# Block products of a two-layer network on one Trainium2 core: part of VectorE's splits and residual adds handed to ScalarE and adding DMAs, two more block pairs, modulation kept off the last tiles

## The chip, the cores and the metric

The kernel runs on one core of one Trainium2 chip. Its engines are named as the profile names them: PE (TensorE; PEld are its weight loads), DVE (VectorE), ACT (ScalarE), POOL (GpSimd) and SP (SyncE, which here issues nearly all DMAs). The metric is the device time of one execution in microseconds (us), as a median over runs.

## The reference, cut to what matters

The network has two layers on 256 latent and 256 context tokens of width 1024. Each layer is a half-weighted gated feed-forward net (ffn), a mixer (a short convolution in layer 0, grouped-query attention in layer 1) and a second ffn. Every step normalises its input, scales and shifts it, and adds its output through a gate. Scale, shift and gate come from a modulation vector, one product per layer of the conditioning vector `c` with a 1024 x 9216 matrix.

```python
mod = (silu(c) @ mod_w[i] + mod_b[i]).reshape(3, 3, 1, 1024)     # shift, scale, gate of three steps
h   = rms(lat, norm_g) * (1 + mod_scale) + mod_shift
gte, up = split(h @ w13, 2)                                       # 1024 -> 2 x 2816
lat = lat + 0.5 * mod_gate * ((silu(gte) * up) @ w2)              # 2816 -> 1024
...                                                               # conv or attention, without the 0.5
```

The context tokens run through the same weights with their own modulation; in layer 1 only the latent tokens are needed after the attention.

## The kernel before, in words

The activations `x` stay in SBUF as 8 tiles of 128 rows (width) by 512 columns (tokens, latent then context). All products are done in a rounded f32 format: `split` (L107 to L109) makes a high part by an ACT copy and a low part by a DVE subtraction, and `mm3` (L128 to L133) multiplies high by high, high by low and low by high, three matmuls for each product.

An ffn with 512 tokens goes through its 22 hidden tiles in thirds of 8, 7 and 7. For each third come first the products with `w13` and the gate (`ffn`, L754), then `project` (L569), which multiplies by `w2` and adds the eight output tiles into `x` through `finish` (L547), two DVE operations for each tile (L553), one for each token stream. After the third third the tiles go on to `tail`, which squares them, sums the squares and prepares the next norm. Tiles 6 and 7 come last and by halves (`late`). There are three ffns with 512 tokens: (0,0), (0,1) and (1,0); the last, (1,1), has 256 tokens and another form.

A hidden tile of the first product is done in one of two ways. As it is: `w13_mm`, 48 matmuls of 512 columns. Or as a `Pair` (L675): seven block products instead of eight, made of sums of weight blocks and of activation blocks (A11, A12, S1 to S4, A22 against B or T1 to T4), 7 x 12 = 84 matmuls of 256 columns. A pair's weights are loaded by SP (two loads of 512 KB); `sums` (L696) forms S1 to S4 on DVE in place and splits all blocks. A22, the fourth product block, keeps its parts in `w4h` and `w4l` (two buffers each); they are used by `four`, a pair's last twelve matmuls, which run after the first products of the next pair. `AS_IS` (L25) says which tiles of the first third stay as they are; in ffn (0,0) tiles 3 to 7 do (tiles 0 to 2 are part of the written-out start), in the others none is named. At the end of a third the last pair's products `seven` and `four` are put between the first tiles of `project`.

The modulation vector is computed on DVE in 224 units (`mod_unit`, L162): an elementwise product with a running sum of a 128 x 1024 tile of the matrix (`junk`), fed by SP loads of `in_modT`, two loads of 512 KB for four units. `tick(n)` makes n units due; it is called behind each pair, as-is tile, output tile and in the attention stage. `mod_ready` runs all units that a vector still lacks. `gate_of` and `lazy_gate` fetch a whole gate at the first `finish` and multiply it by 0.5 for an ffn.

The start and the attention are written out by hand. Elsewhere a scheduler decides each engine's order, so the units of a `tick` needn't stand where it is called. Every engine's queue is run in order.

Of the kernel before, what the change touches and what calls it, by code (L numbers as in the profile page):

```python
# [9 lines left out]
F32 = mybir.dt.float32  # L10
# [11 lines left out]
NM = 22  # L22
THIRDS = (8, 7, 7)

AS_IS = {(0, 0): range(3, 8), (0, 1): (), (1, 0): ()}  # L25

EARLY = 4
HEADS = 8
# [19 lines left out]
def hybrid_kernel(ctx: ExitStack, tc: tile.TileContext, a: dict, out: bass.AP):  # L48
# [13 lines left out]
    def nm(s):  # L62
        uid[0] += 1
        return f"{s}{uid[0]}"
# [102 lines left out]
    def mod_unit(l, ch, pair, raw, j, v):  # L167

        mt = mod_tile(l, ch)
        kt = pair * 2 + j  # L170
        col = ch * KT + kt
        junk = mp.tile([P, D], BF16, name=nm("junk"), tag="junk", bufs=1)
        nc.vector.tensor_tensor_reduce(  # L173
            out=junk,
            in0=raw[j],
            in1=scbc[:, v, :],
            scale=1.0,
            scalar=modb[:, l, col : col + 1],
            op0=ALU.mult,
            op1=ALU.add,  # L180
            accum_out=mt[:, kt, v : v + 1],
        )
        done[l, ch] += 1

    def streams(l, ch):
        return 1 if l == 1 and ch >= 5 else 2
# [23 lines left out]
    def tick(n):  # L210

        owed[0] += n
        while (jobs or units) and owed[0] >= 1:
            owed[0] -= 1
            next_unit()

    def mod_ready(l, ch):
        while not ((l, ch) in done and done[l, ch] == 8 * streams(l, ch)):
            next_unit()
        return modv[l, ch]  # L220
# [10 lines left out]
        return t  # L231

    def gate_of(l, j):
        m = mod_ready(l, 3 * j + 2)
        if j == 1:
            return m
        t = const.tile([P, KT, 2], F32, name=f"G{l}{j}", tag=f"G{l}{j}")
        nv = 1 if (l, j) == (1, 2) else 2
        nc.vector.tensor_scalar(
            out=t[:, :, :nv], in0=m[:, :, :nv], scalar1=0.5, scalar2=None, op0=ALU.mult  # L240
        )
        return t


    accs = {}
# [299 lines left out]
        return tail  # L545

    def finish(m, ps, c0, c1, gate, tail, wide=False):  # L547
        g = gate()
        for s in range(2):
            for o in [s * S - c0] if not wide else range(0, T2 if s == 0 else 0, S):  # L550
                if not c0 <= s * S < c1:
                    continue
                nc.vector.scalar_tensor_tensor(  # L553
                    out=x[:, m, s * S : s * S + S],
                    in0=ps[:, o : o + S],
                    scalar=g[:, m, s : s + 1],
                    in1=x[:, m, s * S : s * S + S],
                    op0=ALU.mult,
                    op1=ALU.add,
                )  # L560
        if tail:
            tail(m, c0, c1)
# [6 lines left out]
    def project(ws, src, nk, gate, tail, tot, late, ev, between=()):  # L569

        def products(ps, w, ks, c0, c1, wide=True):
            ms = [src(k, c0, c1) for k in ks]
            if wide and len(ms[0]) == 3:
                return mm_wide(ps, [w(k) for k in ks], ms, ks[0] == 0, ks[-1] == nk - 1)
            for k, m in zip(ks, ms):  # L580
                mm3(ps[:, : c1 - c0], w(k), m[:2], k == 0, k == nk - 1)

        nf = 3 if between else 2
        ahead = {}

        def get(m):
            for i in range(m, min(m + 3, KT)):
                if i not in ahead:
                    ahead[i] = ws(i)
            return ahead[m]  # L590

        w2 = [get(m) for m in range(nf)]
        p2 = [psum("py") for _ in range(nf)]
        cut = nk - 2 if between else nk - 1
        for i in range(nf):
            products(p2[i], w2[i], range(cut), 0, tot)
            if i < len(between):
                between[i]()
        if between:
            for i in range(nf):  # L600
                products(p2[i], w2[i], (nk - 2,), 0, tot)
        for i in range(nf):
            products(p2[i], w2[i], (nk - 1,), 0, tot)
            finish(i, p2[i], 0, tot, gate, tail, len(src(0, 0, tot)) == 3)
            tick(ev)

        for m in range(nf, KT - late):
            if tail and tot == S and m == KT - 2:
                ready()
            w = get(m)  # L610
            ps = psum("py")
            wide = len(src(0, 0, tot)) == 3 and m < KT - 1
            products(ps, w, range(nk), 0, tot, wide)
            finish(m, ps, 0, tot, gate, tail, wide)
            tick(ev)
        if late:

            wl = [get(m) for m in (6, 7)]
            if tail:
                ready()  # L620
            for s in range(2):
# [53 lines left out]
    class Pair:  # L675
# [4 lines left out]


        def __init__(self, src, h):
            self.h, self.w = h, {}
            self.raw = [load_raw(src[:, c : c + 1024]) for c in (0, 1024)]
            ts = half()
            for i, key in enumerate(("A11", "A12")):
                self.w[key] = [t[:, i * T2 : i * T2 + T2] for t in ts]
                split(*self.w[key], self.raw[i][:, T2:])
# [7 lines left out]
        def sums(self, n):  # L696

            r1, r2 = self.raw
            s1, s2 = r1[:, :T2], r1[:, T2:]
            tt = nc.vector.tensor_tensor  # L700
            if n == 0:
                tt(out=s1, in0=s1, in1=r2[:, :T2], op=ALU.subtract)
                tt(out=s2, in0=s2, in1=s1, op=ALU.subtract)
                self.keep(("S1", "S2"), r1)
                return
            self.w["A22"] = [
                wp.tile([P, T2], F32R, name=nm(t), tag=t, bufs=2) for t in ("w4h", "w4l")
            ]
            split(*self.w["A22"], r2[:, :T2])
            v = lambda t: t.rearrange("p (a c) -> p a c", a=2)  # L710
            tt(  # L711
                out=v(r2), in0=v(r2), in1=s2.unsqueeze(1).to_broadcast([P, 2, T2]),
                op=ALU.subtract,
            )
            self.keep(("S3", "S4"), r2)
# [35 lines left out]
            nc.vector.tensor_tensor(out=self.gm, in0=self.sg, in1=self.u, op=ALU.mult)  # L751
            split(g[0], g[1], self.gm)

    def ffn(l, b, h, tot, gate, tail, gs=(), ev=1.5, z=None):  # L754
        gs = list(gs)
        i0 = 0
        for t, n in enumerate(THIRDS):
            between = ()
            if tot == T2:
# [22 lines left out]
                for i in range(len(gs), n):  # L782
                    if t == 0 and not heads and i in AS_IS[l, b]:
# [12 lines left out]
                        w13_mm(pp, w, h, range(4, KT), 0, T2)  # L796
                        gs.append(new_pair("g"))
                        w13_post(pp, gs[-1], 0, T2)
                        tick(4)
                        continue  # L800
                    if heads:
                        pr = heads.pop(0)
# [44 lines left out]
            def ws2(m):  # L847
# [10 lines left out]
                ws2,  # L858
                (lambda k, c0, c1: cur[k]) if tot == S
                else lambda k, c0, c1: (cur[k][0][:, c0:c1], cur[k][1][:, c0:c1]), n,  # L860
                gate, tail if end else None, tot, 2 if end and tot == T2 else 0, ev, between,
            )
            gs = []

    def lazy_gate(l, j):
        box = []

        def get():
            if not box:
                box.append(gate_of(l, j))  # L870
            return box[0]

        return get


    h = Plain()
# [170 lines left out]
    for i in range(3):  # L1047
        gs0.append(new_pair("g"))
        w13_post(pps[i], gs0[i], 0, T2)

    with tc.issue_after(rows["last"]):
        convk = cload("convk", [P, 3, KT])
        qg = cload("qg", [P, 1])
        kg = cload("kg", [P, 1])
        cosT = cload("cosT", [P, S])
        sinT = cload("sinT", [P, S])


    hn = Plain()
    ffn(0, 0, h, T2, lazy_gate(0, 0), tail_norm(0, 1, hn), gs0, 2)  # L1060
    h = hn

    zs = []
    for m in range(KT):
# [4 lines left out]
        for c0, c1 in ((0, S), (S, T2)) if m == 0 else ((0, T2),):  # L1069
# [11 lines left out]
        u = tp.tile([P, T2], F32, name=nm("u"), tag="gm", bufs=3)  # L1081
        nc.vector.tensor_tensor(out=u, in0=xv, in1=pc, op=ALU.mult)
        d = tp.tile([P, T2], F32, name=nm("d"), tag="gm", bufs=3)
        nc.vector.tensor_scalar(
            out=d, in0=u, scalar1=convk[:, 1, m : m + 1], scalar2=None, op0=ALU.mult
        )
# [11 lines left out]
        nc.vector.tensor_tensor(out=z, in0=d, in1=pb, op=ALU.mult)  # L1098
        zs.append(new_pair("z"))
        split(zs[m][0], zs[m][1], z)  # L1100
        tick(5)

    def by_pairs(key, box=None):
        box = box or {}
# [9 lines left out]
    hn = Blocks()  # L1114
    project(
        by_pairs("cw_out"), lambda k, c0, c1: (zs[k][0][:, c0:c1], zs[k][1][:, c0:c1]), KT,
        lazy_gate(0, 1), tail_norm(0, 2, hn), T2, 2, 1.5,
    )
    h = hn
    hn = Blocks()  # L1120
    ffn(0, 1, h, T2, lazy_gate(0, 2), tail_norm(1, 0, hn), (), 1.7)
    h = hn


    hn = Plain()
    ffn(1, 0, h, T2, lazy_gate(1, 0), tail_norm(1, 1, hn), (), 1.5)
    h = hn
    ap = ctx.enter_context(tc.tile_pool(name="ap", bufs=2))

# [210 lines left out]
    with tc.manual_schedule(engines={e.engine for e in (nc.tensor, nc.vector, nc.scalar, nc.gpsimd)}):  # L1340
# [29 lines left out]
    hn, hz = Beside(), Early()  # L1370
    roomy.append(True)
    project(
        by_pairs("wo", wos), lambda k, c0, c1: aos[k], KT, lazy_gate(1, 1), tail_early(1, 2, hn, hz), S, 0, 0,
    )
    ffn(
        1, 1, hn, S, lazy_gate(1, 2),
        lambda m, c0, c1: nc.sync.dma_start(out[m], x[:, m, :S]), z=hz,
    )

# [79 lines left out]
```

## Time and profile before

| | |
|---|---|
| median of three runs | 1569.89 us (1569.86, 1569.89, 1573.92) |
| the profiled execution | 1571.47 us, of which 1569.7 are the span |
| granted clock of PE, mean | 0.998 |
| PE busy | 1557.7 us, 99% of the span, 10210 matmuls |
| DVE busy | 1333.4 us, 85%, 2129 instructions |
| ACT busy | 733.8 us, 47%, 1213 instructions |
| POOL busy | 25.4 us, 2%, 20 instructions |
| DMA | 248.80 MB, mean 159 GB/s |

The busy share is an average over stages. Where an engine is not the last that the next step waits for, its idle or busy time says nothing of the end. In the rows of the profile, a line such as `L109 DVE TENSOR_TENSOR wl<-wr,wh 128x1024` is an operation of line 109 on DVE that writes `wl` from `wr` and `wh`. Behind it stand the count, the busy time in all, the mean in ns, and the idle time of the engine just before with what ended it. In a window row, each engine has its busy time and its count of instructions; PEclk is the granted clock of PE as a share of full speed.

### The profile page before, as it was taken

To read this page: it belongs to the slowest core of one execution; us is meant where nothing else is said; L and a number is where in the kernel's file an instruction comes from. 1 tells how busy PE (TensorE), PEld (TensorE's weight loads), DVE (VectorE), ACT (ScalarE), POOL (GpSimd) and SP (SyncE) were. 2 spreads that over 40 slices of the span, in tenths; PEclk is the share of its full clock that TensorE was granted. 3 is DMA by queue.
4 is the path that set the end of the run, shared out by engine and by line. 5 is a ranking of instruction groups with operands and counts; after the bars stand their busy time and mean duration, and the time that the engine had idled before them with its cause. 6 is when DMAs were issued, how large, how long until landed. Compare 5 with 4: busy or idle time off the path is not lost.

```text
span 1569.7 us, 25671 instructions
## 1 busy us (share of the span) xinstructions
PE 1557.7 (99%) x10210; PEld 1422.0 (91%) x10210; DVE 1333.4 (85%) x2129; ACT 733.8 (47%) x1213; POOL 25.4 (2%) x20
## 2 busy tenths in 40 slices
PE   9999999999999999999999999999999999999999
PEld 7888998999888899989899899999899889898888
DVE  5998789899997698978989989969978887887676
ACT  5622452545322365435345465435345445674553
POOL 0000000000000000000000000000000002300000
PEclk9999999999999999999999999999999999999999
DMA  9675246355565323542533614533733853366562
GB/s 373 224 237 180 89 132 187 107 173 159 194 209 166 114 75 108 177 146 87 189 126 117 196 41 135 187 108 118 239 112 114 265 154 106 123 207 221 171 199 75
DMA packets 72120, 248.80 MB, mean 159 GB/s; under 512 B 9024, under 2 KB 10816, under 8 KB 72000
## 3 DMA queue, kind: packets, MB, share of 16 engines
q1 hardware_dynamic: 69408, 245.40, 48.0%
q10 hardware_dynamic: 2592, 1.76, 0.4%
q8 instruction: 80, 1.31, 0.3%
q14 instruction: 40, 0.33, 0.1%
HBM read 244.77 MB, written 1.05 MB: 157 GB/s over the span
## 4 chain that ended last, share of the span: by engine, by line
PE 88%; DVE 6%; DMA 2%; ACT 2%; issue 1%; POOL 0%; POOLq 0%; SPq 0%; ACTq 0%; DVEq 0%
PE py L131 8%; PE py L132 8%; PE py L133 8%; PE p L131 6%; PE p L133 6%; PE p L132 6%; PE q L133 5%; PE q L131 4%; PE q L132 4%; PE py L139 2%; PE pu L139 2%; PE pg L139 2%; PE pg L132 1%; PE pg L133 1%; DMA wr<-in_w 1%; PE pu L132 1%
## 5 line engine op out<-in xcount | busy, mean ns | idle before, releaser
L108 ACT ACTIVATE wh<-wr 128x1024 fp32r<-128x1024 f32 (+2 forms) x442 | 393.7, 916 | 361.9 <-PE py L132 119.6
L109 DVE TENSOR_TENSOR wl<-wr,wh 128x1024 fp32r<-128x1024 f32 (+2 forms) x442 | 454.5, 1048 | 95.1 <-ACT wh L108 76.2
L173 DVE CUSTOM_DVE_ANT_0 junk<-wr,scbc,modb 128x1024 bf16<-128x1024 f32 x218 | 279.4, 1282 | 15.2 <-DMA wr<-in_modT 13.1
L131 PE MATMUL py<-gh,wh 128*128 128x512 f32 (+1 forms) x570 | 214.7, 377 | 0.0
L132 PE MATMUL py<-gl,wh 128*128 128x512 f32 (+1 forms) x570 | 214.0, 375 | 0.0
L133 PE MATMUL py<-gh,wl 128*128 128x512 f32 (+1 forms) x570 | 213.9, 375 | 0.0
L133 PEld LDWEIGHTS py<-gh,wl 128*128 128x128 f32 x570 | 108.3, 190 | 19.0
L131 PEld LDWEIGHTS py<-gh,wh 128*128 128x128 f32 x570 | 108.5, 190 | 18.4
L132 PEld LDWEIGHTS py<-gl,wh 128*128 128x128 f32 x570 | 108.5, 190 | 18.2
L131 PE MATMUL p<-th,wh 128*128 128x256 f32 x432 | 122.3, 283 | 0.0
L132 PE MATMUL p<-tl,wh 128*128 128x256 f32 x432 | 122.3, 283 | 0.0
L133 PE MATMUL p<-th,wl 128*128 128x256 f32 x432 | 122.2, 283 | 0.0
L553 DVE SCALAR_TENSOR_TENSOR x<-py,G,x 128x256 f32<-128x256 f32 x189 | 83.5, 479 | 36.3 <-PE py L133 25.1
L133 PE MATMUL q<-bh,wl 128*128 128x256 f32 x320 | 91.5, 286 | 0.1
L131 PE MATMUL q<-bh,wh 128*128 128x256 f32 x320 | 90.9, 284 | 0.4 <-ACT wh L108 0.4
L132 PE MATMUL q<-bl,wh 128*128 128x256 f32 x320 | 90.5, 283 | 0.0
L132 PEld LDWEIGHTS p<-tl,wh 128*128 128x128 f32 x432 | 82.8, 192 | 0.3
L131 PEld LDWEIGHTS p<-th,wh 128*128 128x128 f32 x432 | 82.8, 192 | 0.3
L133 PEld LDWEIGHTS p<-th,wl 128*128 128x128 f32 x432 | 82.8, 192 | 0.0
L108 ACT ACTIVATE w4h<-wr 128x512 fp32r<-128x512 f32 x54 | 33.8, 625 | 75.1 <-DMA wr<-in_w 56.9
L108 ACT ACTIVATE gh<-gm 128x512 fp32r<-128x512 f32 x66 | 41.6, 630 | 56.0 <-DVE gm L751 53.8
L711 DVE TENSOR_TENSOR wr<-wr,wr 128x1024 f32<-128x1024 f32 x54 | 66.0, 1222 | 0.7
(303 smaller groups left out, 3946.3 us busy)
## 6 DMA issues: line engine op xcount, KB each, us to landing
wr<-in_w SPq DMA_DIRECT2D x176, 512.0 KB, 4.5
wr<-in_modT SPq DMA_DIRECT2D x122, 512.0 KB, 4.5
wr<-in_w2b SPq DMA_DIRECT2D x64, 448.0 KB, 3.9
wr<-in_w2a SPq DMA_DIRECT2D x32, 512.0 KB, 4.7
pm<-in_mod SPq DMA_DIRECT2D x16, 512.0 KB, 10.2
wr<-in_cw_cx SPq DMA_DIRECT2D x16, 512.0 KB, 4.7
wr<-in_cw_b SPq DMA_DIRECT2D x8, 512.0 KB, 4.4
wr<-in_cw_out SPq DMA_DIRECT2D x8, 512.0 KB, 3.9
```

Source lines behind the costliest of these rows:

```text
L108: nc.scalar.activation(out=hi, in_=src, func=AF.Copy)
L109: return nc.vector.tensor_tensor(out=lo, in0=src, in1=hi.bitcast(F32), op=ALU.subtract)
L131: nc.tensor.matmul(ps, wh, mh, start=first, stop=False, **kw)
L132: nc.tensor.matmul(ps, wh, ml, start=False, stop=False, **kw)
L133: nc.tensor.matmul(ps, wl, mh, start=False, stop=last, **kw)
L139: nc.tensor.matmul(ps, w[0], m[2], start=first and n == 0, stop=False)
L173: nc.vector.tensor_tensor_reduce(out=junk, in0=raw[j], in1=scbc[:, v, :], scale=1.0, scalar=modb[:, l, col : col + 1], op0=ALU.mult, op1=A ...
L553: nc.vector.scalar_tensor_tensor(out=x[:, m, s * S : s * S + S], in0=ps[:, o : o + S], scalar=g[:, m, s : s + 1], in1=x[:, m, s * S : s * ...
L711: tt(out=v(r2), in0=v(r2), in1=s2.unsqueeze(1).to_broadcast([P, 2, T2]), op=ALU.subtract,)
```

## The change

1. Tiles 6 and 7 of the first third of ffn (0,0) become pairs; 56 pairs in all, 54 before.
2. A pair's `w4l` is no longer subtracted by DVE. ACT writes minus the high part, and a DMA issued by POOL adds the weights from memory to it (256 KB).
3. In the first two thirds of the three large ffns, output tiles 0 to 5 are no longer added by DVE. ACT scales the two halves of the product into a tile `gy`, and a DMA issued by POOL adds that to `x` (256 KB); 36 tiles in all.
4. The 0.5 of the gates is put into the modulation units of channels 2 and 8 and, once, into their bias. A gate is fetched tile by tile: only the units up to the tile in hand are forced.
5. The last output tiles (from tile 6, or from tile 5 where the last tiles go by halves) make no unit due; the rates of the others and of the other calls of `tick` are changed.
6. One scaling in the convolution goes from DVE to ACT, eight times.

```diff
-AS_IS = {(0, 0): range(3, 8), (0, 1): (), (1, 0): ()}
+AS_IS = {(0, 0): range(3, 6), (0, 1): (), (1, 0): ()}
...
-            scale=1.0,
+            scale=0.5 if ch in (2, 8) else 1.0,
...
     def gate_of(l, j):
-        m = mod_ready(l, 3 * j + 2)
...
+        ch = 3 * j + 2
+        def get(m):
+            while done.get((l, ch), 0) < (m // 2 + 1) * 2 * streams(l, ch):
+                next_unit()
+            return modv[l, ch]
+        return get
...
     def finish(m, ps, c0, c1, gate, tail, wide=False):
-        g = gate()
+        g = gate(m)
+        if c1 - c0 == T2 and not tail and m < 6:
+            t = tp.tile([P, T2], F32, name=nm("gy"), tag="sg" if m % 2 else "gm", bufs=3)
+            for s in range(2):
+                d = slice(s * S, s * S + S)
+                nc.scalar.activation(
+                    out=t[:, d], in_=ps[:, d], func=AF.Copy, scale=g[:, m, s : s + 1]
+                )
+            nc.gpsimd.dma_start(out=x[:, m, :], in_=t, accum_op=ALU.add)
+            return
...
             finish(m, ps, 0, tot, gate, tail, wide)
-            tick(ev)
+            if m < (5 if late else 6):
+                tick(ev)
...
-            split(*self.w["A22"], r2[:, :T2])
+            w4h, w4l = self.w["A22"]
+            nc.scalar.activation(out=w4h, in_=r2[:, :T2], func=AF.Copy)
+            nc.scalar.activation(out=w4l, in_=w4h.bitcast(F32), func=AF.Copy, scale=-1.0)
+            nc.gpsimd.dma_start(out=w4l, in_=self.src[:, 1024 : 1024 + T2], accum_op=ALU.add)
...
-                        tick(4)
+                        tick(3)
...
+    for ch in (2, 8):
+        b = modb[:, :, ch * KT : ch * KT + KT]
+        nc.vector.tensor_scalar(out=b, in0=b, scalar1=0.5, scalar2=None, op0=ALU.mult)
...
-    ffn(0, 0, h, T2, lazy_gate(0, 0), tail_norm(0, 1, hn), gs0, 2)
+    ffn(0, 0, h, T2, gate_of(0, 0), tail_norm(0, 1, hn), gs0, (2.9, 2.4))
...
-        nc.vector.tensor_scalar(
-            out=d, in0=u, scalar1=convk[:, 1, m : m + 1], scalar2=None, op0=ALU.mult
-        )
+        nc.scalar.activation(out=d, in_=u, func=AF.Copy, scale=convk[:, 1, m : m + 1])
...
-        tick(5)
+        tick(4)
...
-        lazy_gate(0, 1), tail_norm(0, 2, hn), T2, 2, 1.5,
+        gate_of(0, 1), tail_norm(0, 2, hn), T2, 2, 1.8,
...
-    ffn(0, 1, h, T2, lazy_gate(0, 2), tail_norm(1, 0, hn), (), 1.7)
+    ffn(0, 1, h, T2, gate_of(0, 2), tail_norm(1, 0, hn), (), (2.7, 2))
...
-    ffn(1, 0, h, T2, lazy_gate(1, 0), tail_norm(1, 1, hn), (), 1.5)
+    ffn(1, 0, h, T2, gate_of(1, 0), tail_norm(1, 1, hn), (), (2.5, 1.6))
```

The two rates of an ffn are for its first two thirds and for its last.

More of the change, by code (lines that the diff above doesn't have):

```diff
@@ L233, in gate_of @@
     def gate_of(l, j):
-        m = mod_ready(l, 3 * j + 2)
[L235 to L238, printed above, removed]
-        nc.vector.tensor_scalar(
-            out=t[:, :, :nv], in0=m[:, :, :nv], scalar1=0.5, scalar2=None, op0=ALU.mult
-        )
-        return t
+        ch = 3 * j + 2
[4 more added lines that the diff above has]
+        return get
     accs = {}
@@ L682, in __init__ @@
         def __init__(self, src, h):
-            self.h, self.w = h, {}
+            self.h, self.w, self.src = h, {}, src
             self.raw = [load_raw(src[:, c : c + 1024]) for c in (0, 1024)]
@@ L752, in four, with ffn @@
             split(g[0], g[1], self.gm)
-    def ffn(l, b, h, tot, gate, tail, gs=(), ev=1.5, z=None):
+    def ffn(l, b, h, tot, gate, tail, gs=(), ev=(0, 0), z=None):
         gs = list(gs)
@@ L860, in ffn @@
                 else lambda k, c0, c1: (cur[k][0][:, c0:c1], cur[k][1][:, c0:c1]), n,
-                gate, tail if end else None, tot, 2 if end and tot == T2 else 0, ev, between,
+                gate, tail if end else None, tot, 2 if end and tot == T2 else 0, ev[end], between,
             )
             gs = []
[L865 to L873, printed above, removed]
     h = Plain()
@@ L1083, in hybrid_kernel @@
         d = tp.tile([P, T2], F32, name=nm("d"), tag="gm", bufs=3)
-        nc.vector.tensor_scalar(
-            out=d, in0=u, scalar1=convk[:, 1, m : m + 1], scalar2=None, op0=ALU.mult
-        )
+        nc.scalar.activation(out=d, in_=u, func=AF.Copy, scale=convk[:, 1, m : m + 1])
         u2 = u.rearrange("p (s t) -> p s t", s=2)
@@ L1372, in hybrid_kernel @@
     project(
-        by_pairs("wo", wos), lambda k, c0, c1: aos[k], KT, lazy_gate(1, 1), tail_early(1, 2, hn, hz), S, 0, 0,
+        by_pairs("wo", wos), lambda k, c0, c1: aos[k], KT, gate_of(1, 1), tail_early(1, 2, hn, hz), S, 0, 0,
     )
     ffn(
-        1, 1, hn, S, lazy_gate(1, 2),
+        1, 1, hn, S, gate_of(1, 2),
         lambda m, c0, c1: nc.sync.dma_start(out[m], x[:, m, :S]), z=hz,
```

## The prediction

> **What bounds the kernel now.** I read the page's busy shares and chain first, then windows of single stages, then the waits, then the timeline at the worst gap.
>
> ```profile
> span 1569.7 us, 25671 instructions
> PE 1557.7 (99%) x10210; PEld 1422.0 (91%) x10210; DVE 1333.4 (85%) x2129; ACT 733.8 (47%) x1213; POOL 25.4 (2%) x20
> PE 88%; DVE 6%; DMA 2%; ACT 2%; issue 1%; POOL 0%; POOLq 0%; SPq 0%; ACTq 0%; DVEq 0%
> ```
>
> PE (TensorE) is busy in 1557.7 of 1569.7 us, so all the time in which it waits is 12 us. DVE (VectorE) at 85% is not the bound: what is taken off it is worth only those PE waits that it caused.
>
> ```profile
> core 0: us, PE busy (x) PEld busy (x) DVE busy (x) ACT busy (x) POOL busy (x), PEclk, DMA share, GB/s
> 50.00:100.00 50.00, 50.00 (x222) 41.42 (x221) 49.54 (x74) 24.41 (x34) 0.00 (x0) 1.00 0.63 204
> 100.00:150.00 50.00, 50.00 (x222) 41.38 (x222) 47.54 (x75) 12.88 (x16) 0.00 (x0) 1.00 0.68 210
> 700.00:750.00 50.00, 50.00 (x419) 50.00 (x418) 38.63 (x54) 27.72 (x48) 0.00 (x0) 1.00 0.30 91
> 1255.00:1270.00 15.00, 13.34 (x83) 12.85 (x82) 9.20 (x22) 5.64 (x12) 0.00 (x0) 0.77 0.37 118
> ```
>
> Even where DVE is busy for 49.54 of 50 us, in the first ffn, PE is busy for all 50. The first two windows hold 512-column matmuls only: 50/222 = 0.2252 us each. The third holds 256-column ones: 50/419 = 0.1193 us each. The last is the tail of the first ffn of layer 1: PE is idle for 1.66 us, and a clock of 0.77 over 15 us loses about 3.45 us more. This one place holds some 5.1 us. Its timeline:
>
> ```profile
> 1246.24 0.88 DVE L553 SCALAR_TENSOR_TENSOR x<-py,G,x 128x256 f32<-128x256 f32 x2 [1.17 <-PE py L133]
> ...
> 1250.24 1.28 DVE L173 CUSTOM_DVE_ANT_0 junk<-wr,scbc,modb 128x1024 bf16<-128x1024 f32 x1
> ...
> 1251.56 2.25 SPq L104 DMA_DIRECT2D wr<-in_modT  x2
> ...
> 1256.91 1.28 DVE L173 CUSTOM_DVE_ANT_0 junk<-wr,scbc,modb 128x1024 bf16<-128x1024 f32 x1 [2.39 <-DMA wr<-in_modT]
> 1258.13 0.42 DVE L259 TENSOR_TENSOR acc<-acc,sq 128x256 f32<-128x256 f32 x1
> 1258.60 0.38 PE L268 MATMUL ss<-ones,acc 128*128 128x1 f32 x2 [1.52 <-DVE acc L259]
> ```
>
> A modulation unit (junk, L173) stands in DVE's queue ahead of the last addition of squares. Its load could only be issued at 1251.56, once the unit of 1250.24 had freed its buffer; DVE waits 2.39 us for it, and PE waits for DVE. The remaining waits of weight are these:
>
> ```profile
> ACT w4h L108 <- DMA wr<-in_w: 56.9, 16, 9.6
> ...
> PEld q L133 <- DVE wl L109: 1.5, 7, 0.3
> ...
> PEld q L131 <- ACT wh L108: 1.3, 4, 0.6
> PE pg L132 <- DVE bl L109: 1.3, 2, 1.0
> ```
>
> So splits that come late in the pairs cost PE 1.5 us by DVE (seven times) and 1.3 us by ACT (ScalarE); the first product after a norm waits for `bl` twice.
>
> **The change part by part.**
>
> *Two more block pairs.* Hidden tiles 6 and 7 of the first third change from 48 matmuls of 512 columns (48 x 0.2252 = 10.81 us) to 84 of 256 (84 x 0.1193 = 10.02 us): 0.79 us each, **-1.6 us** on the path. This has one answer as long as PE stays fed.
>
> *A22's low part by ScalarE and DMA (L723, L724), 56 times, and six residual tiles by ScalarE and DMA (L557), 36 times.*
>
> ```profile
> L109 DVE TENSOR_TENSOR w4l<-wr,w4h 128x512 fp32r<-128x512 f32 x54 | 37.1, 687 | 1.2 <-ACT w4h L108 1.0
> L108 ACT ACTIVATE w4h<-wr 128x512 fp32r<-128x512 f32 x54 | 33.8, 625 | 75.1 <-DMA wr<-in_w 56.9 <-PE p L132 18.2
> L553 DVE SCALAR_TENSOR_TENSOR x<-py,G,x 128x256 f32<-128x256 f32 x189 | 83.5, 479 | 36.3 <-PE py L133 25.1 <-PE py L141 10.8
> L734 ACT COPY gm<-q 128x256 f32<-128x256 f32 x54 | 19.7, 365 | 41.2 <-PE q L133 41.2
> L711 DVE TENSOR_TENSOR wr<-wr,wr 128x1024 f32<-128x1024 f32 x54 | 66.0, 1222 | 0.7
> L173 DVE CUSTOM_DVE_ANT_0 junk<-wr,scbc,modb 128x1024 bf16<-128x1024 f32 x218 | 279.4, 1282 | 15.2 <-DMA wr<-in_modT 13.1
> ```
>
> DVE loses 54 x 0.687 = 37.1 us and 72 x 0.479 = 34.5 us. The two new pairs give some back: I count a pair at eight 128x512 operations (0.687), three of 128x1024 (1.222) and one of 128x256 (near 0.43), 9.6 us, or 8.9 without the low part; an as-is tile has two of each, 3.8 us. That is 5.1 us each, 10 us in all. DVE ends about 61 us lighter, near 1272 us, less the eight conv scalings that go to ACT. ACT gains 56 x 0.625 = 35 us, 72 copies x 0.365 = 26 us, eight conv scalings at about 0.625 = 5 us, and some 5 for the pairs: near 805 us, or 51% of the span. None of it is on PE's path by itself.
>
> What the relief is worth: at most the late splits, 1.5 + 1.3 = 2.8 us; at least nothing, as these waits stand at the starts of thirds and partly come from ACT, which gets more. I take half of DVE's share, **-0.7 us**.
>
> What the DMAs cost: the trace has no accumulating transfer and no DMA issued by POOL, so it is bounded by rows on both sides.
>
> ```profile
> 1199.71 0.62 ACT L108 ACTIVATE w4h<-wr 128x512 fp32r<-128x512 f32 x1
> 1201.53 0.68 DVE L109 TENSOR_TENSOR w4l<-wr,w4h 128x512 fp32r<-128x512 f32 x1
> 1216.75 0.28 PE L133 MATMUL p<-th,w4l 128*128 128x256 f32 x1
> wr<-in_w SPq DMA_DIRECT2D x176, 512.0 KB, 4.5
> pm<-in_mod SPq DMA_DIRECT2D x16, 512.0 KB, 10.2
> ```
>
> This pair has the least cover of the 54: 16.4 us from the end of the w4h copy (1200.3) to the first matmul that uses w4l. A second copy (0.63) leaves 15.8 us for the transfer. A plain transfer of twice the size lands in 4.5 us, and the slowest kind, queued at the start, in 10.2. Hence **0**, with 5 to 11 us to spare. If that cover is gone, each of the 47 pairs that follow another pair in their third pays what is over 15.8. The accumulated x is read only in the next third, 70 us or more later, so its landing costs nothing.
>
> The new waits: on POOL, a w4l transfer waits for its ACT copy, and the residual transfers issued later queue behind it; nobody needs those soon. On ACT, the w4h copy already waits up to 9.6 us for a load; the w4l copy and the residual copies now queue there, and a residual copy holds one of six PSUM buffers until it has run. A tile of the second product takes 21 to 24 matmuls, 24 x 0.2252 = 5.4 us, so three spare buffers cover about 16 us, more than 9.6: 0. The new tiles share the sg and gm buffers (three each) with the pairs; a pair's `head` comes many us after the last residual tile: 0. The 92 transfers move 24 MB beside 248.8, where the DMA share is 0.30 to 0.68; loads that land later have cover where the queue runs ahead: 0, a few us at worst (third rival).
>
> *Modulation off the last tiles; rates; gates.* The units are as many as before (224), and so are their loads on SP's queue; they move to earlier tiles of the same stage, past w13 and w2 loads that run ahead anyway. The 0.5 folded into the unit saves a few tiny DVE operations. What is gained is in the tails. Conv's out projection has four units in its tail before, and none after:
>
> ```profile
> 550.96 1.28 DVE L173 CUSTOM_DVE_ANT_0 junk<-wr,scbc,modb 128x1024 bf16<-128x1024 f32 x1 [0.48 <-DMA wr<-in_modT]
> ...
> 554.50 1.28 DVE L173 CUSTOM_DVE_ANT_0 junk<-wr,scbc,modb 128x1024 bf16<-128x1024 f32 x1
> ...
> 555.15 0.30 PEld L268 LDWEIGHTS ss<-ones,sq 128*128 128x128 f32 x2 [0.24 <-ACT sq L251]
> ```
>
> The PE wait seen there is 0.24 us; with the `bl` waits (1.3 on PE over two places, whose order stays) the bounds are 0 and 1.5; I take the near row, **-0.3 us**. The tail at 1251 to 1258 is not cleared: its units don't come from the ffn's own ticks but from the attention stage's, which the change leaves alone and the scheduler pulls forward. In the changed kernel's order DVE again has two units, two residual adds, a split, two additions of squares, one residual add, then a unit whose load on SP waits for the second unit's buffer, then the last addition. DVE is tied to PE just before (it waits 1.17 us for a product at 1246.24), so a lighter DVE doesn't start these units sooner. I leave the 5.1 us where they are.
>
> **Sum**: -1.6 - 0.7 - 0.3 = -2.6 us on the profiled execution's 1571.47, 1568.9 us. That execution lies 1.6 us over the median of the three runs (1569.89), so the forecast is **1567.3 us**. By the bounds: from 1568.3 (pairs only) to 1564.0 (-1.6 - 2.8 - 1.5); small new waits at ACT, as large as those gained, would give up to 1571.
>
> **The rivals.**
>
> *B, the tail of layer 1's first ffn is mended as well.* The 2.39 us wait vanishes if the unit's load is issued 2.4 us sooner or the unit falls behind the addition; then 5.1 us more go: 1569.89 - 2.6 - 5.1 = 1562.2. If the wait only gets shorter, the clock may stay full: -3.45, 1563.8. For it: fewer units owed at the end, and a lighter DVE. Against it: the order above. On the clock the Trainium skill ("TensorE: Matmul & The Clock Gate", Part 1) says that the clock halves after an idle window of about 3.4 us; the trace disagrees, with a loss of 3.45 us behind an idle time of 1.66 us. By that page the loss need not come back; by the row it does. Chance 0.26.
>
> *C, the accumulating transfers are late (slower).* One place: w4l at a pair's last four products. It decides at 15.8 us from POOL's issue to landing. Against it are the 4.5 and 10.2 us rows; for it, that these are another kind of transfer, behind other work in POOL's queue, in stages where DVE is at 49.54 of 50 us and DMA at 0.63 to 0.68. If a dozen pairs of the busy first ffn are 1 us late, PE loses 12 us: 1567.3 + 12 = 1579; if all 47 are, 1614. The Trainium skill speaks here against the change ("SBUF — State Buffer", SBUF: two separate sides): POOL-issued DMAs have their descriptors written by GpSimd, which is locked out while DVE runs certain two-port operations, plain f32 copies among them. No run here shows it yet; DVE's work here is nearly all with two tensor inputs. Chance 0.21.
>
> *D, the edits do nothing but the pairs.* The DVE relief is all off the path: 1568.3, inside the forecast's own range.
>
> **How the numbers follow.** About 0.3% (4.7 us) is what a measurement of this kernel can tell from no change: faster is under 1565.2, slower over 1574.6. The forecast with D has 0.53, of which 0.04 lies under 1565.2 (all bounds together); B adds 0.26 there; C's 0.21 is slower. Faster 0.30, same 0.49, slower 0.21. The likeliest case's own range is 1564.0 to 1571; the full one reaches down to B's 1562.2, less 0.7 for more of the late splits, 1561.5, and up to the mild end of C, eight pairs late by 1 us, 1575.5; C's worse part, under 0.2, is left out.
>
> **What would show it.** Right: L131 to L133 with 168 more 256-column matmuls and 96 fewer of 512; DVE near 1272, ACT near 805 us; 92 POOL transfers landing under 11 us; no PE wait named w4l; the 2.4 us wait on in_modT and a clock under 0.8 still in the tail near 1253; none at 555. Wrong: PE waiting for w4l or for a DMA (C), the clock at 1.00 through 1250 to 1270 (B), or PE idle at places that had none.

## The result, and the profile after

The changed kernel takes 1610.3 us (median of four runs, 1609.52 to 1612.95) beside 1571.9 of the kernel before on the same chip: a ratio of 1.0247, 95% interval 1.0224 to 1.0270. It is slower by some 39 us where 2.6 us less were forecast. The page of its profiled execution, in the lines that answer to those shown of before, with the two lines of the chain and the queue that is new (q0, POOL's transfers):

```profile
span 1607.7 us, 26138 instructions
...
PE 1564.5 (97%) x10282; PEld 1432.0 (89%) x10282; DVE 1282.2 (80%) x2007; ACT 800.5 (50%) x1361; POOL 106.0 (7%) x112
...
q1 hardware_dynamic: 69408, 245.40, 47.0%
q0 software_dynamic: 13248, 24.12, 8.8%
...
PE 61%; DVE 16%; DMA 13%; issue 5%; ACT 4%; POOL 0%; POOLq 0%; ACTq 0%; DVEq 0%; SPq 0%
DMA wr<-in_w 7%; DVE wl L109 5%; DMA wr<-in_modT 5%; DVE junk L173 4%; PE p L131 4%; PE p L132 4%; PE p L133 4%; PE py L131 4%; PE py L132 4%; PE py L133 4%; PE q L131 3%; PE q L133 3%; PE q L132 3%; PE py L139 2%; PE pu L139 2%
```

DVE fell and ACT rose as counted. Yet the chain, which was 88% PE, now runs through DVE and loads for 29% of the span: a lighter DVE waits more, and PE behind it. PE's gaps are new in six places. In the windows around them (columns as in the windows of before):

```profile
core 0: us, PE busy (x) PEld busy (x) DVE busy (x) ACT busy (x) POOL busy (x), PEclk, DMA share, GB/s
150.00:175.00 25.00, 20.40 (x121) 18.53 (x120) 18.38 (x26) 7.96 (x13) 0.86 (x1) 0.93 0.41 108
270.00:290.00 20.00, 14.56 (x88) 13.31 (x87) 16.59 (x25) 6.78 (x11) 0.92 (x2) 0.89 0.57 166
700.00:718.00 18.00, 14.81 (x93) 13.63 (x92) 12.87 (x19) 6.65 (x11) 0.88 (x1) 0.94 0.44 126
814.00:836.00 22.00, 14.14 (x86) 13.04 (x85) 17.80 (x26) 6.78 (x11) 0.86 (x1) 0.83 0.54 140
1066.00:1084.00 18.00, 16.23 (x96) 14.78 (x96) 14.21 (x22) 5.22 (x8) 0.16 (x1) 0.92 0.38 107
1180.00:1200.00 20.00, 16.74 (x98) 15.61 (x98) 15.31 (x23) 7.57 (x13) 0.89 (x1) 0.84 0.59 162
sum 123.00, PE 96.89 PEld 88.91 DVE 95.17 ACT 40.96 POOL 4.57; mean PE 16.15 PEld 14.82 DVE 15.86 ACT 6.83 POOL 0.76
```

PE is idle for 123.00 - 96.89 = 26.1 us, and what the clock lacks of 1.00, times the length of each window, comes to 13.4 us more: 39.5 us, near the 38.0 by which the span grew. The kernel before, in the 50 us around four of these places:

```profile
150.00:200.00 50.00, 50.00 (x375) 48.09 (x374) 35.98 (x50) 23.38 (x39) 0.00 (x0) 1.00 0.26 84
250.00:300.00 50.00, 50.00 (x337) 46.40 (x336) 45.99 (x70) 20.08 (x33) 0.00 (x0) 1.00 0.47 151
800.00:850.00 50.00, 49.96 (x412) 49.60 (x411) 43.23 (x64) 26.42 (x46) 0.00 (x0) 1.00 0.37 113
1150.00:1200.00 50.00, 50.00 (x413) 49.73 (x412) 39.37 (x56) 26.41 (x46) 0.00 (x0) 1.00 0.36 111
```

Each place is the start of a third that follows a `project` with residual transfers, two in each of the three large ffns. These rows of the waits name it, first before (L702 and L703 are the lines L713 and L714 of the changed kernel):

```profile
ACT wh L108 <- DVE wr L703: 49.7, 28, 5.7
...
DVE wr L702 <- DMA wr<-in_w: 12.6, 13, 1.9
```

and after:

```profile
ACT wh L108 <- DVE wr L714: 125.6, 43, 9.7
...
DVE wr L713 <- DMA wr<-in_w: 69.6, 39, 4.9
...
PE q L131 <- ACT gm L749: 26.5, 7, 7.9
```

PE waits for a small copy on ScalarE, 26.5 us in seven waits. The kernel before has no such row. One of the six in the timeline:

```profile
812.07 0.69 DVE L713 TENSOR_TENSOR wr<-wr,wr 128x512 f32<-128x512 f32 x1 [4.89 <-DMA wr<-in_w]
...
814.58 1.28 DVE L173 CUSTOM_DVE_ANT_0 junk<-wr,scbc,modb 128x1024 bf16<-128x1024 f32 x1 [1.21 <-DMA wr<-in_modT]
...
816.99 1.28 DVE L173 CUSTOM_DVE_ANT_0 junk<-wr,scbc,modb 128x1024 bf16<-128x1024 f32 x1
...
818.31 17.68 SPq L104 DMA_DIRECT2D wr<-in_w  x6
```

```profile
828.18 0.69 DVE L713 TENSOR_TENSOR wr<-wr,wr 128x512 f32<-128x512 f32 x1 [3.17 <-DMA wr<-in_w]
...
831.58 1.06 ACT L108 ACTIVATE wh<-wr 128x1024 fp32r<-128x1024 f32 x1 [9.71 <-DVE wr L714]
...
832.54 0.35 ACT L749 COPY gm<-q 128x256 f32<-128x256 f32 x1
832.95 0.58 PE L131 MATMUL q<-bh,wh 128*128 128x256 f32 x1 [7.86 <-ACT gm L749]
```

Read it backwards. At 832.95 PE goes on once the copy at 832.54 has run. That copy stood in ScalarE's queue behind a split that waited 9.71 us for DVE's sums of the next pair; DVE waited for that pair's load. SP had issued nothing since its modulation loads (two, ending at 804.8) until 818.31, just as the unit of 816.99 had ended and given a buffer of the ring back. That unit's own load had taken 11.3 us (803.23 to 814.55). How late loads are in this stretch shows beside the same stretch of the kernel before (DMA issues: count, size, median us to landing), first before, from 772 to 817 us:

```profile
wr<-in_w SPq DMA_DIRECT2D x12, 512.0 KB, 4.1
wr<-in_modT SPq DMA_DIRECT2D x1, 512.0 KB, 4.5
```

and after, from 790 to 835 us:

```profile
q0 software_dynamic: 1152, 2.10, 27.8%
...
wr<-in_w SPq DMA_DIRECT2D x11, 512.0 KB, 6.0
x<-gy POOLq DMA_DIRECT2D x6, 256.0 KB, 8.6
wr<-in_modT SPq DMA_DIRECT2D x2, 512.0 KB, 12.0
w4l<-in_w POOLq DMA_DIRECT2D x2, 256.0 KB, 8.3
```

Eight transfers of POOL hold 27.8% of the DMA engines' time there for 2.10 MB. The two modulation loads take 12.0 us in place of 4.5. Two windows of the changed kernel show both steps (columns as above, DMA share the last but one):

```profile
797.00:817.00 20.00, 20.00 (x90) 16.57 (x89) 11.62 (x20) 7.67 (x14) 5.22 (x6) 1.00 1.00 253
817.00:818.30 1.30, 1.30 (x8) 1.07 (x7) 1.30 (x4) 1.13 (x2) 0.00 (x0) 1.00 0.06 11
```

For 20 us the DMA engines are busy all the time, and what is loaded then lands late. Then they stand nearly idle, because SP waits for a buffer of the ring.

### The profile page after: what moved, and what is told of

Same layout as the page of the kernel before. It is cut to its first block, busy times and chain, and to the rows that moved or that the text cites. A ratio compares the mean times of both kernels' runs of the same rounds, so it can differ in the third digit from the quotient of the medians.

```text
span 1607.7 us, 26138 instructions
## 1 busy us (share of the span) xinstructions
PE 1564.5 (97%) x10282; PEld 1432.0 (89%) x10282; DVE 1282.2 (80%) x2007; ACT 800.5 (50%) x1361; POOL 106.0 (7%) x112
## 3 DMA queue, kind: packets, MB, share of 16 engines
q1 hardware_dynamic: 69408, 245.40, 47.0%
## 4 chain that ended last, share of the span: by engine, by line
PE 61%; DVE 16%; DMA 13%; issue 5%; ACT 4%; POOL 0%; POOLq 0%; ACTq 0%; DVEq 0%; SPq 0%
DMA wr<-in_w 7%; DVE wl L109 5%; DMA wr<-in_modT 5%; DVE junk L173 4%; PE p L131 4%; PE p L132 4%; PE p L133 4%; PE py L131 4%; PE py L132 4%; PE py L133 4%; PE q L131 3%; PE q L133 3%; PE q L132 3%; PE py L139 2%; PE pu L139 2%
## 5 line engine op out<-in xcount | busy, mean ns | idle before, releaser
L173 DVE CUSTOM_DVE_ANT_0 junk<-wr,scbc,modb 128x1024 bf16<-128x1024 f32 x214 | 274.3, 1282 | 42.2 <-DMA wr<-in_modT 40.1
L131 PE MATMUL p<-th,wh 128*128 128x256 f32 x448 | 126.8, 283 | 0.0
L132 PE MATMUL p<-tl,wh 128*128 128x256 f32 x448 | 126.8, 283 | 0.0
L133 PE MATMUL p<-th,wl 128*128 128x256 f32 x448 | 126.8, 283 | 0.0
L724 POOL DMA_DIRECT2D w4l<-in_w x56 | 49.0, 875 | 991.7 <-ACT w4l L723 869.7
L713 DVE TENSOR_TENSOR wr<-wr,wr 128x512 f32<-128x512 f32 x56 | 38.7, 691 | 69.6 <-DMA wr<-in_w 69.6
L756 ACT ACTIVATE sg<-sg 128x512 f32<-128x512 f32 x56 | 35.4, 632 | 94.1 <-DVE sg L755 93.9
L563 DVE SCALAR_TENSOR_TENSOR x<-py,mod,x 128x256 f32<-128x256 f32 x141 | 63.7, 479 | 21.2 <-PE py L141 10.4
```

The costliest lines, as they stand in the source:

```text
L131: nc.tensor.matmul(ps, wh, mh, start=first, stop=False, **kw)
L132: nc.tensor.matmul(ps, wh, ml, start=False, stop=False, **kw)
L133: nc.tensor.matmul(ps, wl, mh, start=False, stop=last, **kw)
L173: nc.vector.tensor_tensor_reduce(out=junk, in0=raw[j], in1=scbc[:, v, :], scale=0.5 if ch in (2, 8) else 1.0, scalar=modb[:, l, col : col ...
L563: nc.vector.scalar_tensor_tensor(out=x[:, m, s * S : s * S + S], in0=ps[:, o : o + S], scalar=g[:, m, s : s + 1], in1=x[:, m, s * S : s * ...
L724: nc.gpsimd.dma_start(out=w4l, in_=self.src[:, 1024 : 1024 + T2], accum_op=ALU.add)
```

## The experiments

Every edit lets the scheduler place instructions anew, so small differences between variants also hold a change of order. "Late loads" counts SP's loads into the ring between 50 and 1250 us that took over 7 us; the kernel before has 1. The count shows where lateness is, not what it costs: 25 late loads go with 11 us of loss in one variant and 30 with 24 in another.

| kernel | median, us | ratio to before (95%) | late loads |
|---|---|---|---|
| changed kernel | 1610.3 | 1.0247 (1.0224 to 1.0270) | 29 |
| residual by DVE | 1572.4 | 1.0011 (0.9997 to 1.0024) | 5 |
| low part by DVE | 1594.1 | 1.0153 (1.0118 to 1.0188) | 30 |
| old modulation | 1594.9 | 1.0154 (1.0131 to 1.0177) | 24 |
| before + residual alone | 1580.8 | 1.0072 (1.0048 to 1.0095) | 25 |
| gy copies, DVE adds | 1580.5 | 1.0059 (1.0039 to 1.0080) | 9 |
| plain transfer | 1594.9 | 1.0151 (1.0133 to 1.0169) | 18 |
| first three tiles | 1594.6 | 1.0132 (1.0110 to 1.0155) | 28 |
| last three tiles | 1588.0 | 1.0115 (1.0086 to 1.0144) | 14 |
| copy first on ACT | 1606.8 | 1.0231 (1.0216 to 1.0247) | 26 |
| 16 of 128 rows | 1579.3 | 1.0063 (1.0044 to 1.0082) | 10 |
| no modulation loads | 1580.9 | 1.0064 (1.0044 to 1.0085) | 6 |
| before, no modulation loads | 1572.0 | 1.0016 (1.0003 to 1.0028) | 2 |
| no adding transfer | 1573.8 | 1.0028 (1.0015 to 1.0041) | 0 |
| before + pairs alone | 1572.8 | 1.0017 (1.0007 to 1.0026) | 0 |
| before + pairs + tail | 1567.7 | 0.9982 (0.9970 to 0.9994) | 0 |
| before + tail | 1568.0 | 0.9989 (0.9979 to 0.9998) | 2 |

**Which part: residual, low part or modulation.** First the residual by DVE again:

```diff
-        if c1 - c0 == T2 and not tail and m < 6:
+        if False:
```

> The changed kernel, with the residual tiles added by DVE again (no gy copies, no transfers into x). In the changed kernel PE loses about 39 us of start-to-start gaps at six places, each the first pair of the third that follows a project with residual transfers. Theory R (the residual transfers, 36, share the DMA engines with the next third's loads and make them late): the six stalls go, about 1570 us. Theory W (the 56 transfers into w4l do it): about 1605 to 1610, stalls stay. Theory M (the modulation units moved into the first five tiles by the new rates do it): about 1605 to 1610.

1572.4 us: the six stalls are gone. Then the low part by DVE:

```diff
-            nc.scalar.activation(out=w4l, in_=w4h.bitcast(F32), func=AF.Copy, scale=-1.0)
-            nc.gpsimd.dma_start(out=w4l, in_=self.src[:, 1024 : 1024 + T2], accum_op=ALU.add)
+            split(w4h, w4l, r2[:, :T2])
```

> The changed kernel, with w4l subtracted by DVE again (no adding transfer from memory). Theory R: the stalls stay, 1600 to 1612 us. Theory W: they go, about 1570. Theory M: they stay, about 1610.

1594.1 us, below the range of theory R. The old calls of `tick`:

```diff
-            if m < (5 if late else 6):
-                tick(ev)
+            tick(ev)
...
-    ffn(0, 0, h, T2, gate_of(0, 0), tail_norm(0, 1, hn), gs0, (2.9, 2.4))
+    ffn(0, 0, h, T2, gate_of(0, 0), tail_norm(0, 1, hn), gs0, (2, 2))
```

> The changed kernel with the old calls of tick: also behind the last tiles, and at the old rates (2, 1.7, 1.5; convolution 5 and 1.5; as-is tiles 4). Both kinds of adding transfer stay. Theory R and theory W: the six stalls stay, 1600 to 1615 us. Theory M: they go, about 1570.

1594.9 us. And the residual transfers put into the kernel before, the code of `finish` as in the change:

> The kernel before, with nothing but the residual tiles by ScalarE and adding transfers (36). Theory R: the six stalls appear, 1595 to 1612 us. Theory W and theory M: about the time before, within 5 us.

1580.8 us. So no theory held as it was written. The residual transfers are needed for the loss, but alone they make 11 of its 39 us; without the low part's transfers, or with the old modulation, 24 and 25 are left. Together the parts cost more than the sum of each alone: the last two cost almost nothing where the first is missing (1572.4).

**What of the residual step.** The copies kept, DVE adds:

```diff
-            nc.gpsimd.dma_start(out=x[:, m, :], in_=t, accum_op=ALU.add)
+            nc.vector.tensor_tensor(out=x[:, m, :], in0=x[:, m, :], in1=t, op=ALU.add)
```

> The changed kernel, with the 36 residual tiles still scaled by ScalarE into gy, but added to x by one DVE operation each in place of the transfer. Theory R1 (the transfers on the DMA engines make the next third's loads late; ScalarE then waits for DVE, DVE for a load, and PE waits for a copy queued on ScalarE behind that): the six stalls go, 1568 to 1576 us. Theory R2 (the 72 copies on ScalarE, and the order that the scheduler gives them, are enough): the stalls stay, 1595 to 1612.

1580.5 us, 4.5 over R1's range and far from R2's: some 30 us hang on the transfer, and 8 on the copies and the order that comes with them. A transfer that doesn't add:

```diff
-            nc.gpsimd.dma_start(out=x[:, m, :], in_=t, accum_op=ALU.add)
+            nc.vector.tensor_tensor(out=t, in0=x[:, m, :], in1=t, op=ALU.add)
+            nc.gpsimd.dma_start(out=x[:, m, :], in_=t)
```

> The changed kernel, with gy added to x by DVE into gy and then copied to x by a plain transfer from POOL: as many transfers of the same size at the same places, none of them adding. If the adding is what costs DMA time (theory R1a), the loads land near their usual 4.6 us and the stalls mostly go: 1570 to 1582 us. If any transfer issued there does it (R1b): 1595 to 1612. R2: 1595 to 1612, and x1 as slow.

1594.9 us, at the lower edge of R1b's range and far from R1a's: a plain transfer costs 14 us more than DVE's addition alone (1580.5), and the adding costs another 15. The page rows of q0 fit this: without residual transfers, with plain ones, with adding ones.

```profile
q0 software_dynamic: 8064, 14.68, 5.5%
```

```profile
q0 software_dynamic: 10944, 24.12, 6.9%
...
x<-gy POOLq DMA_DIRECT2D x36, 256.0 KB, 5.6
```

```profile
q0 software_dynamic: 13248, 24.12, 8.8%
...
w4l<-in_w POOLq DMA_DIRECT2D x56, 256.0 KB, 5.7
x<-gy POOLq DMA_DIRECT2D x36, 256.0 KB, 7.6
```

In engine time (share x 16 x span) that is 1384, 1758 and 2264 us: a plain transfer holds 10 us of it, an adding one 24. A load of 512 KB holds 26, by q1's row (47.0% for 245.40 MB). An adding transfer of half the bytes costs the DMA engines as much as a whole load. The Trainium skill ("Collectives: The Full Stack", The bandwidth ceiling: the fold count and why AG ≠ RS ≠ AR) says of the collective ReduceScatter that its add needs two source reads and gets about half the rate; the ratio measured in this kernel's transfers is 2.4.

Half of the tiles, first the early ones, then (with 3 <= m < 6) the late ones:

```diff
-        if c1 - c0 == T2 and not tail and m < 6:
+        if c1 - c0 == T2 and not tail and m < 3:
```

> The changed kernel with residual transfers for the output tiles 0 to 2 only (18, which come in a burst of three), tiles 3 to 5 by DVE. Theory R1: the burst meets the loads of the next third's first pairs, which were issued at 796 to 804 us beside transfers at 796 to 798: more than half of the 38 us stay, 1592 to 1608. If the later, single ones do it: 1572 to 1585.

> The changed kernel with residual transfers for the output tiles 3 to 5 only (18, singly), tiles 0 to 2 by DVE. Theory R1 with the burst: less than half of the 38 us, 1573 to 1588. If the later ones do it: 1592 to 1608.

1594.6 and 1588.0 us, 24 and 18 us over before by the medians. The first lies within R1's range and the second at the upper edge of it, but the intervals of the two ratios overlap, so it isn't shown that the burst is worse. Over 1572.4, where no tile goes by transfer, the halves cost 22 and 16 us, together as much as all six tiles (38). Then the same number of transfers with an eighth of the bytes:

```diff
-            nc.gpsimd.dma_start(out=x[:, m, :], in_=t, accum_op=ALU.add)
+            nc.gpsimd.dma_start(out=x[:16, m, :], in_=t[:16], accum_op=ALU.add)
```

> The changed kernel, with each residual transfer cut to 16 of 128 rows (the rest of the sum is left out): as many transfers, copies and waits, an eighth of the bytes. Theory R1 (the DMA time of the transfers makes loads late): near the variant that adds by DVE, 1574 to 1584 us. Rival (their number, POOL's queue and the order do it): 1597 to 1612.

1579.3 us, as R1 has it: for some 30 of the 39 us it is the bytes' DMA time that costs, not the number of transfers or POOL's queue.

**How lateness reaches PE.** ScalarE's splits of a pair held behind the copy of the pair before it:

```diff
-            nc.scalar.copy(self.gm[:, S:], self.q1)
+            self.copied = nc.scalar.copy(self.gm[:, S:], self.q1).ins
...
-                        pr.sums(0)
-                        pr.sums(1)
+                        with tc.issue_after(prev.copied) if prev else ExitStack():
+                            pr.sums(0)
+                            pr.sums(1)
```

> The changed kernel, with ScalarE's splits of a pair's weights kept behind the copy of the pair before it (gm, L749), by order alone. In the changed kernel PE waits 26.5 us for that copy, which stands in ScalarE's queue behind a split whose load is late. Theory H (the loss is head-of-line blocking on ScalarE): that wait goes; PE then runs on until it needs the late weights themselves, 4.3 us of matmuls later, so roughly half of the loss goes: 1585 to 1598 us. Rival (PE would wait for the late weights anyway, as long): 1605 to 1612.

1606.8 us. The wait named gm fell to a few us, but the time came back as many small waits for late splits and for DVE's additions:

```profile
PEld p L131 <- DVE p L760: 9.2, 15, 0.9
...
PEld q L133 <- DVE wl L109: 7.3, 11, 2.0
...
PEld q L131 <- ACT gm L749: 4.3, 8, 1.0
```

Theory H fell, as far as this run can tell: ScalarE's queue says where PE waits, not how long. (The order may cost something of its own, too, since splits now start later in every pair; no run separates that.) Then the modulation loads left out, in the changed kernel and in the one before:

```diff
-            return [load_raw(src[:, j * D : j * D + D]) for j in range(2)]
+            return [scbc[:, j, :] for j in range(2)]
```

> The changed kernel, with the modulation units of the stages up to the attention reading a tile that is already there: their loads are left out, and with them their places in the ring of weight buffers. Theory R1 with the ring (late modulation loads hold DVE and the ring, so the next pair's loads are issued late): nearly all of the loss goes, 1565 to 1575 us, and its control within 5 us of that. Rival (the transfers delay the pairs' loads by themselves): 1585 to 1605.

> The kernel before, with the same modulation loads left out: the control for the run above. By the 5.1 us of the tail near 1257, where DVE waits for such a load: 1562 to 1567 us.

1580.9 and 1572.0 us: some 30 of the 39 us go with these loads. The run takes away two things at once, their places in the ring and 62 MB of traffic (q1 moves 183.52 MB in place of 245.40), and nothing here tells how much each is worth. The profiled execution took 1574.2 us, 6.7 less than the median, so it shows only part of what is left, mostly at the two first places:

```profile
150.00:175.00 25.00, 23.36 (x157) 21.48 (x156) 24.86 (x37) 8.71 (x16) 0.86 (x1) 1.00 0.32 96
270.00:290.00 20.00, 15.66 (x117) 15.41 (x116) 19.58 (x32) 7.36 (x13) 0.00 (x0) 0.91 0.31 106
```

There DVE is busy all the time (24.86 of 25 us, 19.58 of 20), so another limit may have taken over there. The expectation (1565 to 1575) was missed by 6 us, and the control was 0.16% slower than before (0.03 to 0.28), where the tail should have made it 3 to 8 us faster; why is open.

**The terms that should have gained.** Neither kind of adding transfer, both edits above together:

> The changed kernel without both kinds of adding transfer: residual tiles and w4l by DVE as before; the two pairs, the modulation, the gates and the convolution's scaling as changed. With the residual by DVE alone it took 1572.4 against 1569.8. If the transfers into w4l cost something of their own: 1568 to 1570. If the moved modulation does: 1572 to 1576.

1573.8 us, in the range that was given to the moved modulation; but the pairs alone, next, make most of these 4 us. In the kernel before nothing but the pairs:

```diff
-AS_IS = {(0, 0): range(3, 8), (0, 1): (), (1, 0): ()}
+AS_IS = {(0, 0): range(3, 6), (0, 1): (), (1, 0): ()}
```

> The kernel before, with tiles 6 and 7 of the first third as pairs and nothing else. The prediction's term: 1.6 us less than before (1568.2 beside 1569.8). If DVE's 10 us more in that stage are felt: up to 3 us more than before.

1572.8 us, slower by 0.17% (0.07 to 0.26). Three windows of it:

```profile
8.00:23.00 15.00, 13.72 (x104) 10.54 (x102) 6.70 (x20) 7.16 (x15) 0.00 (x0) 0.77 1.00 381
100.00:110.00 10.00, 8.82 (x74) 8.62 (x73) 9.72 (x15) 4.50 (x9) 0.00 (x0) 1.00 0.51 163
1255.00:1275.00 20.00, 17.09 (x112) 16.38 (x110) 12.45 (x29) 8.37 (x17) 0.00 (x0) 0.83 0.41 129
```

At the new pairs PE is idle for 1.18 us, in one wait for a copy on ScalarE behind a split that waits for DVE's sums, with DVE busy for 9.72 of 10 us. In the kernel before DVE is as busy there (9.74), but PE isn't idle. So that wait takes back most of the 1.6 us that the block products save. The profiled execution took 1575.9 us, 3.1 more than the median; the rest of what it loses on the profile of before is in the old tail, where one wait now lasts 2.8 us in place of 1.5, and in a clock of 0.77 from 8 to 23 us, where the profile of before has 1.00. With that tail cleared:

```diff
-    tick(1)
+    with tc.issue_after(normed[0]):
+        tick(1)
```

(`normed[0]` is the norm's last DVE operation; so, too, for the other four calls in the attention stage)

> The kernel before with the two pairs, and the attention stage's modulation units queued on DVE behind the last operation of the norm ahead of it. Rival B's price for the tail near 1253 to 1270 was 5.1 us (1.66 idle, 3.45 of clock): with the pairs 6.7 less than before, about 1563. If the units only move the wait to another place: 1566 to 1570.

> The kernel before with the attention stage's modulation units queued on DVE behind the norm ahead of it, and nothing else. With the two pairs the same step took 5.1 us off (1572.8 to 1567.7); from 1569.7 that gives about 1564.6 us. If the gain belongs to the pairs' kernel only: 1568 to 1570.

1567.7 us with the pairs, 1568.0 without: the only versions that beat both kernels, by 0.18% (0.06 to 0.30) and 0.11% (0.02 to 0.21). Neither gains the 5.1 us that the tail was priced at over the kernel before. In the tail of the second PE is now idle for 0.7 us and keeps its clock:

```profile
core 0: us, PE busy (x) PEld busy (x) DVE busy (x) ACT busy (x) POOL busy (x), PEclk, DMA share, GB/s
1255.00:1270.00 15.00, 14.31 (x114) 13.68 (x113) 10.82 (x26) 7.68 (x18) 0.00 (x0) 1.00 0.13 40
```

## Why the prediction was wrong, point by point

- **DMA cost, the step that failed.** "Loads that land later have cover where the queue runs ahead: 0, a few us at worst" was 36 to 38 us: 1610.3 beside 1573.8 without both kinds of transfer and 1572.4 without the residual's, some 30 of it by the residual transfers' DMA time. The prediction's own sign of being wrong, PE idle at places that had none, came. I asked when each transfer's own result is needed, and there the working held: w4l landed in 5.7 us (median; 10.6 at most) against a cover of 15.8, no PE wait is named after it, and nobody waited for `x`. I priced the 92 transfers by their bytes (24 MB beside 248.8), not by their DMA time (8.8% beside 47.0%), and I didn't ask what the other transfers in the same window are needed for. The loads of the next third's pairs and of the modulation are the ones that came late; they share one ring of eight buffers, which SP fills in order, so one late load delays the issue of the next.
- **The queue on SP.** "Past w13 and w2 loads that run ahead anyway" failed with it. Moving the units off the last tiles put more of their loads beside the residual transfers: by the times of issue and landing, 10 modulation loads overlap such a transfer, 3 with the old calls. With those calls 15 us of the loss go.
- **Rival C** had the right side, and a time near the result by luck: its place, w4l, is not where PE waits. Its port rule from the Trainium skill ("SBUF — State Buffer", SBUF: two separate sides) isn't seen to act, though no run tests it alone: plain transfers from POOL landed in 5.6 us (median) in a run with DVE 82% busy.
- **Pairs, -1.6.** The matmuls count as forecast, but alone the pairs cost about 2.7 us; with the tail cleared they gain about 0.3 over the same kernel without them, within the runs' uncertainty. "One answer as long as PE stays fed" was the condition that failed there: PE waited 1.18 us. In the changed kernel, whose DVE has less to do, PE stays fed at the new pairs, so the term may well hold in it; no run measures it there:

```profile
95.00:115.00 20.00, 20.00 (x158) 19.51 (x157) 17.59 (x25) 10.65 (x17) 0.00 (x0) 1.00 0.54 182
```

- **DVE's relief, -0.7, and the tails, -0.3.** DVE came to 1282 us (forecast 1272) and ACT to 800 (805), and no gain of it is seen. No run has the whole relief without the transfers' cost. The nearest pair is the low part alone handed over (1572.4 us, DVE 1309) beside neither part (1573.8, DVE 1341), and their intervals overlap. The upper bound of the relief, 2.8 us, was read from weight loads (PEld), which overlap PE; of the two waits that it sums, PE's own rows before have little more than the one below. Of the tails' gain nothing is seen either: without the adding transfers the rest of the change is slower than before by 0.28% (0.15 to 0.41), of which the pairs alone make 0.17%.

```profile
PE q L131 <- ACT wh L108: 0.4, 1, 0.4
```

- **The tail at 1251 to 1270** kept its stall, as said (PE waits 1.59 us for the addition near 1300 in the changed kernel). The price was mis-sized: 5.1 us came from one execution with a halved clock. Clearing the tail gained 5.1 with the pairs, but 1.9 without. The clock comes and goes between executions: of 22 runs of the kernel before, those with a mean granted clock of 1.000 took 1567.0 to 1568.7 us, those with 0.997 or 0.998 took 1570.4 to 1573.3. So the median, from which the forecast starts, holds only part of that loss. In the changed kernel's own profile the same stall costs no clock:

```profile
1296.00:1311.00 15.00, 12.51 (x98) 11.64 (x97) 12.09 (x27) 6.99 (x16) 0.00 (x0) 1.00 0.36 120
```

What stays open: the last 8 to 10 us. The variants with an eighth of the rows, with DVE adding and without modulation loads all end near 1580, not at 1572; the copies on ScalarE, the shared gy buffers or the scheduler's order may hold it, and no run here tells them apart. Why the parts together cost more than each alone is argued from the loads' times and from the ring, which the trace shows at one of the six places; it isn't shown by a run that gave the ring more buffers, which wasn't tried.

## What to carry to other kernels

Price an added transfer by the DMA engine time that it takes (here an adding 256 KB transfer weighed as much as a plain 512 KB load), and then look at every other transfer in flight beside it: the one with the least cover sets the cost, not the added one. Where loads share a ring of buffers that one queue fills in order, a late load can delay the issue of the next, so lateness can grow. A stall that one profile shows with a clock loss behind it is worth its idle time, and the clock only in those executions that lose it.

## What the runs showed of the hardware

An adding transfer from SBUF to SBUF of 256 KB took 24 us of DMA engine time (summed over the 16 engines) against 10 for a plain one, and landed in 7.6 us (median) against 5.6. The clock fell below full after single waits as short as 1.8 us (the window from 1066 us: 1.77 us idle, 0.92 over 18 us), in the kernel before after one of 1.52 us (near 1257, 0.77 over 15 us), and stayed full over a window with 2.5 us idle (from 1296 us). The Trainium skill ("TensorE: Matmul & The Clock Gate", Part 1) gives about 3.4 us of idleness for it, in windows that run freely; the first row disagrees with that length, and that like stalls end differently agrees with the free-running windows. The clock records of the traces show such windows: in the changed kernel the six falls to half clock begin at 169.61, 285.67, 715.75, 828.38, 1080.97 and 1193.61 us, which lie 34, 126, 33, 74 and 33 times 3.413 us apart, and each lasts one to three such periods. In all traces of this case, wherever PE was idle for 1.9 us or more of one period (between 20 and 1500 us), the next ran at half clock; below that some did and some didn't. The 1.77 us near 1080 lie within one period, while of the 2.5 us from 1296 no period holds more than 1.35.
